# A softmax's first store moved from SyncE's queue of transfers to ScalarE's

## The chip, the cores and the metric

One core of one Trainium2 chip. The metric is the device time of one execution in microseconds (us), given as the median of the runs. The other cores are idle.

## The reference

A softmax over the last axis with temperature 2, on 16 x 1024 rows of 512 float32 values:

```python
def reference(x):                       # (16, 1024, 512) float32
    x_scaled = x / 2.0
    x_max = np.max(x_scaled, axis=-1, keepdims=True)
    exp_x = np.exp(x_scaled - x_max)
    return exp_x / np.sum(exp_x, axis=-1, keepdims=True)
```

33.55 MB come in and 33.55 MB go out. With 128 partitions there are 128 rows of 2 KB for each partition.

## The kernel before

All 128 rows per partition are cut into nine tiles of 3, 5, 9, 15, 21, 31, 15, 17 and 12 rows, and these into 23 chunks. A tile is the unit of a transfer, a chunk that of the arithmetic. The packet records have 144 records for each transfer: 128 packets, one per partition with all the tile's rows of that partition (6 to 62 KB), 8 for each of the core's 16 DMA engines, and 16 completions. The transfers of one queue wait in line; this line is called the ring below. An arena of 99 rows holds them; tiles 7 and 8 take the places of earlier ones and wait for their stores. VectorE finds the maximum, ScalarE does the exponential in place and the sum, VectorE takes the reciprocal and multiplies, two chunks behind its maximum. One queue, SyncE's, issues every load and store in a fixed order:

```python
PLAN = [                                # (rows of the chunks of a tile), place in the arena
    ([3], 0), ([5], 3), ([5, 4], 8), ([5] * 3, 17), ([7] * 3, 32), ([8, 8, 8, 7], 53),
    ([5] * 3, 84), ([6, 6, 5], 0), ([4] * 3, 17),
]
QUEUE = [
    ("load", 0), ("load", 1), ("load", 2), ("load", 3), ("load", 4), ("load", 5),
    ("load", 6), ("store", 0), ("store", 1), ("store", 2), ("store", 3), ("load", 7),
    ("store", 4), ("load", 8), ("store", 5), ("store", 6), ("store", 7), ("store", 8),
]
...
            if kind == "load":
                for u in behind.get(t, []):              # tiles whose place it takes
                    nc.sync.wait_ge(st[u], stored[u])
                ... nc.sync.dma_start(out=arena[...], in_=dram(xf, t)[...]).then_inc(ld[t], 16)
                continue
            ...
            nc.sync.wait_ge(s_mul, k + 1)                # the tile's last chunk is multiplied
            ... nc.sync.dma_start(out=dram(of, t)[...], in_=arena[...])
...
        for k, (t, b, c, a) in enumerate(chunks):        # ScalarE
            for r in range(c):
                ins = nc.scalar.activation(... Exp, bias=negmax, scale=0.5, accum_out=sums ...)
                if r == 0:
                    ins._wait_ge(s_max, k + 1)
            ins.then_inc(s_exp, 1)
        for k in range(len(chunks) + LAG):               # VectorE, LAG = 2
            if k < len(chunks):
                do_max(k)
            if k >= LAG:
                do_mul(k - LAG)
```

The softmax here doesn't subtract the row's maximum and nothing guards it: scores larger than these inputs give would overflow.

## Time and profile before

| | before |
|---|---|
| time, median of the 3 runs known at the prediction | 163.24 us (162.96 to 163.44) |
| span of the profiled run | 161.1 us |
| VectorE busy, ScalarE busy | 125.1 us, 94.0 us |
| transfers, all on one queue | 67.11 MB, 97.8% of 16 engines' span |

The list of transfers (what, queue, size, us from issue to landing) has store 0 and load 7:

```profile
out_dram<-arena SPq DMA_DIRECT2D x1, 768.0 KB, 49.0
arena<-in_x_dram SPq DMA_DIRECT2D x1, 4352.0 KB, 19.7
```

Store 0 is on its way for 49 us, because loads 4 to 6 (17.6 MB) and the rest of load 3 stand ahead of it in the same ring. And the chain of who waited for whom has for VectorE (us in total, times, longest):

```profile
DVE negmax L115 <- DMA arena<-in_x_dram: 9.0, 4, 4.5
```

VectorE waits for a load four times, all before 22.2 us, and never again.

### The profile page before, as it was taken

The numbers are of one execution on the slowest core, as the hardware profiler recorded it, in microseconds if no ns is written. First come the engines' busy times: TensorE is split into PE (matmuls) and PEld (weight loads), VectorE is DVE, ScalarE is ACT, GpSimd is POOL, SyncE is SP. The second block draws the span as 40 slices with busy tenths as digits, with TensorE's granted clock in tenths as the row PEclk, the third lists the DMA queues.
The fourth block names the chain that finished last, engine by engine and source line by source line (L and its number), as shares of the span: only waits on it lengthen the run. The fifth ranks groups of instructions, "written<-read, shape, count | busy, mean of one in ns | idle before, by whom it ended". The sixth has DMA issues, their size and how long they took to land.

```text
span 161.1 us, 494 instructions
## 1 busy us (share of the span) xinstructions
DVE 125.1 (78%) x174; ACT 94.0 (58%) x257; POOL 0.2 (0%) x4
## 2 busy tenths in 40 slices
DVE  0557989999999999999999999999999994000000
ACT  3455957674977949696977764697875770000000
POOL 0000000000000000000000000000000000000000
DMA  7999999997996998999999989899899979999991
GB/s 264 458 476 397 458 404 480 450 490 331 504 473 286 458 397 292 458 433 458 419 413 458 480 382 491 363 416 552 349 457 489 426 340 458 409 439 415 420 464 61
DMA packets 2595, 67.13 MB, mean 417 GB/s; under 512 B 288, under 2 KB 288, under 8 KB 544
## 3 DMA queue, kind: packets, MB, share of 16 engines
q1 hardware_dynamic: 2592, 67.11, 97.8%
q14 instruction: 3, 0.02, 0.0%
HBM read 33.55 MB, written 33.55 MB: 416 GB/s over the span
## 4 chain that ended last, share of the span: by engine, by line
DVE 69%; DMA 13%; issue 0%; DVEq 0%; SPq 0%
DVE negmax L115 38%; DVE arena L128 30%; DMA arena<-in_x_dram 13%; DVE recip L124 1%; DVEq L209 0%; SPq L100 0%
## 5 line engine op out<-in xcount | busy, mean ns | idle before, releaser
L141 ACT ACTIVATE arena<-arena,negmax 128x512 f32<-128x512 f32 x128 | 90.7, 709 | 37.1 <-DVE negmax L115 37.1
L115 DVE TENSOR_REDUCE negmax<-arena 128x5 f32<-128x2560 f32 (+5 forms) x23 | 71.7, 3116 | 9.0 <-DMA arena<-in_x_dram 9.0
L128 DVE TENSOR_SCALAR arena<-arena,recip 128x512 f32<-128x512 f32 x128 | 52.8, 482 | 0.8
L141 ACT ACTIVATION_READ_ACCUMULATOR arena<-arena,negmax 128x1 f32 x128 | 23.9, 187 | 0.0
L124 DVE RECIPROCAL recip<-sums 128x5 f32<-128x5 f32 (+5 forms) x23 | 4.2, 181 | 0.0
L141 ACT ACT_TABLE_LOAD x1 | 1.3, 1283 | 1.3 <-PEq L198 1.3
L198 POOL MEMSET const-bfloat16-1.0<- 128x1 bf16 x1 | 0.1, 101 | 0.0
L198 POOL MEMSET const-uint8-127<- 128x1 uint8 x1 | 0.1, 101 | 0.0
L198 POOL MEMSET const-float32-0.0<- 128x1 f32 x1 | 0.1, 98 | 0.2 <-issue 0.2
L198 POOL MEMSET const-float32-1.0<- 128x1 f32 x1 | 0.1, 98 | 0.0
## 6 DMA issues: line engine op xcount, KB each, us to landing
arena<-in_x_dram SPq DMA_DIRECT2D x1, 7936.0 KB, 50.9
out_dram<-arena SPq DMA_DIRECT2D x1, 7936.0 KB, 36.5
arena<-in_x_dram SPq DMA_DIRECT2D x2, 3840.0 KB, 40.8
out_dram<-arena SPq DMA_DIRECT2D x2, 3840.0 KB, 32.5
arena<-in_x_dram SPq DMA_DIRECT2D x1, 5376.0 KB, 32.4
out_dram<-arena SPq DMA_DIRECT2D x1, 5376.0 KB, 32.0
arena<-in_x_dram SPq DMA_DIRECT2D x1, 4352.0 KB, 19.7
out_dram<-arena SPq DMA_DIRECT2D x1, 4352.0 KB, 25.5
```

Source lines behind the costliest of these rows:

```text
L115: nc.vector.reduce_max(out=negmax[:, b : b + c], in_=arena[:, a : a + c], axis=mybir.AxisListType.X, negate=True,)._wait_ge(ld[t], loads_o ...
L124: nc.vector.reciprocal(out=recip[:, b : b + c], in_=sums[:, b : b + c])._wait_ge(s_exp, k + 1).then_inc(s_rec, 1)
L128: ins = nc.vector.tensor_scalar_mul(out=arena[:, a + r], in0=arena[:, a + r], scalar1=recip[:, b + r : b + r + 1],)
L141: ins = nc.scalar.activation(out=arena[:, a + r], in_=arena[:, a + r], func=mybir.ActivationFunctionType.Exp, bias=negmax[:, b + r : b + r ...
L198: nc = _bacc.Bacc("TRN2", target_bir_lowering=False, num_devices=1)
```

## The change

Store 0 need not stand for 45 us behind loads (its first packet starts at 62.6 us). It goes to ScalarE's queue, issued in ScalarE's program after chunk 2's exponentials, so that it runs while SyncE's queue still loads. Its early landing would also be one thing less ahead of load 7. The diff, cut to its core (`do_store` is the old store code with the engine as an argument):

```diff
-    ("load", 6), ("store", 0), ("store", 1), ("store", 2), ("store", 3), ("load", 7),
+    ("load", 6), ("store", 1), ("store", 2), ("store", 3), ("load", 7),
...
+SIDE = {2: 0}
...
+    def do_store(engine, t, lo, hi, groups):
+        ...
+        engine.wait_ge(s_mul, k + 1)
+        ... engine.dma_start(out=dram(of, t)[...], in_=arena[...]) ...
...
             ins.then_inc(s_exp, 1)
+            if k in SIDE:
+                do_store(nc.scalar, SIDE[k], 0, tiles[SIDE[k]][1], [(0, P, 1)])
```

More of the change, by code (lines that the diff above doesn't have):

```diff
@@ L90 @@
             loads_of[t] = loads_of.get(t, 0) + 16 * (len(rest[2]) if rest else 1)
+    def do_store(engine, t, lo, hi, groups):
+        b, r, at = tiles[t]
+        k = max(k for k, c in enumerate(chunks) if c[0] == t and c[1] - b < hi)
+        engine.wait_ge(s_mul, k + 1)
+        for p, q, step in groups:
+            u = t if t in awaited else "end"
+            engine.dma_start(
+                out=dram(of, t)[p:q:step, lo:hi], in_=arena[p:q:step, at + lo : at + hi, :]
+            ).then_inc(st[t] if t in awaited else s_end, 16)
+            stored[u] = stored.get(u, 0) + 16
     def do_queue(items):
@@ L94, in do_queue @@
             b, r, at = tiles[t]
-            lo, hi, groups = rest if rest else (0, r, [(0, P)])
-            if kind == "load":
-                for u in behind.get(t, []):
-                    nc.sync.wait_ge(st[u], stored[u])
-                for p, q in groups:
-                    nc.sync.dma_start(
-                        out=arena[p:q, at + lo : at + hi, :], in_=dram(xf, t)[p:q, lo:hi]
-                    ).then_inc(ld[t], 16)
+            lo, hi, groups = rest if rest else (0, r, [(0, P, 1)])
+            if kind == "store":
+                do_store(nc.sync, t, lo, hi, groups)
                 continue
-            k = max(k for k, c in enumerate(chunks) if c[0] == t and c[1] - b < hi)
-            nc.sync.wait_ge(s_mul, k + 1)
-            for p, q in groups:
-                u = t if t in awaited else "end"
+            for u in behind.get(t, []):
+                nc.sync.wait_ge(st[u], stored[u])
+            for p, q, step in groups:
                 nc.sync.dma_start(
-                    out=dram(of, t)[p:q, lo:hi], in_=arena[p:q, at + lo : at + hi, :]
-                ).then_inc(st[t] if t in awaited else s_end, 16)
-                stored[u] = stored.get(u, 0) + 16
+                    out=arena[p:q:step, at + lo : at + hi, :],
+                    in_=dram(xf, t)[p:q:step, lo:hi],
+                ).then_inc(ld[t], 16)
     def do_max(k):
```

## The prediction

> **What bounds the kernel now.** I read the page's summary first, then the SyncE queue's own waits, then the engines' order of time around 19 us (where the moved store will land), then stretches of the DMA traffic, and last the trace's packet records.
>
> The page, busy shares, the 40 slices and the queues:
>
> ```profile
> span 161.1 us, 494 instructions
> DVE 125.1 (78%) x174; ACT 94.0 (58%) x257; POOL 0.2 (0%) x4
> ...
> DVE  0557989999999999999999999999999994000000
> ...
> DMA  7999999997996998999999989899899979999991
> ...
> q1 hardware_dynamic: 2592, 67.11, 97.8%
> ```
>
> VectorE stops at slice 34, but the DMA row stays at 9 from slice 2 to slice 39: one queue, 97.8% of the 16 engines' span, carries all 67.11 MB. The 2592 packets are 18 transfers of 144 (128 rows of one partition each, and 16 completions). The packet records agree: from 2 to 156 us the number in flight is 16.0 in every 2 us stretch, so every engine moves one packet after the other with no gap. The sum of packet times over 16 engines is 157.8 us. This kernel is bound by transfers; VectorE is not.
>
> The page's chain of what ended last names VectorE all the same (69%), because it ends with the last multiply:
>
> ```profile
> 133.19 0.49 DVE arena L128
> 133.68 0.40 DVEq L209
> 134.07 0.79 DVE arena L128 x2
> ```
>
> That is 134.86 us; the span is 161.1. After it come 26 us of stores already queued or issued at once. So the chain is a false lead here: VectorE may slip until the queue would run dry. Store 8 is issued at 134.89 us, and store 7 ends at 152.5 us (packet records): 17 us in hand. Store 5 is issued at 96.94, and load 8 ahead of it ends at 114.4: again 17 us.
>
> The SyncE queue's own waits:
>
> ```profile
> SPq L108 <- DVE arena L128: 93.3, 8, 16.6
> SPq L98 <- DMA out_dram<-arena: 25.8, 1, 25.8
> SPq L209 <- PEq L209: 25.6, 2, 25.1
> SPq L100 <- DMA out_dram<-arena: 7.8, 1, 7.8
> ```
>
> They look large, but cost nothing: SyncE waits while earlier transfers still run. The 25.8 us are load 7's wait for stores 0 to 2 (it goes out at 74.94 us); store 3, 3.93 MB, is still in the ring and keeps the engines busy until 83.6 us.
>
> One place does lose time. Stretches of 2 us (engine busy times, clock, DMA share, GB/s):
>
> ```profile
> 52.40:54.40 2.00, 1.97 (x7) 1.92 (x5) 0.00 (x0) 1.00 1.07 461
> 54.40:56.40 2.00, 2.00 (x4) 2.00 (x7) 0.00 (x0) 1.00 1.03 445
> 56.40:58.40 2.00, 2.00 (x1) 1.12 (x4) 0.00 (x0) 1.00 1.10 476
> 58.40:60.40 2.00, 1.97 (x4) 0.59 (x1) 0.00 (x0) 1.00 0.96 323
> 60.40:62.40 2.00, 2.00 (x7) 2.00 (x7) 0.00 (x0) 1.00 0.97 246
> 62.40:64.40 2.00, 2.00 (x2) 2.00 (x7) 0.00 (x0) 1.00 0.76 316
> 64.40:66.40 2.00, 2.00 (x1) 1.16 (x4) 0.00 (x0) 1.00 1.09 461
> ```
>
> From 59 to 64 us the engines are busy but slow. The packet records put it down to the last two packets per engine of load 6, just ahead of store 0, the kernel's first store: the 128 packets of load 6 take 1.292 us in the mean against a median of 1.138, so 8 x 0.154 = 1.23 us per engine are lost. The next two passages from a load to a store (load 7 to store 4, load 8 to store 5) lose 0.13 and 0.05 us, and those from a store to a load nothing. Why the first one is dear the trace doesn't say; that it is the first store of the kernel is my guess, by likeness to load 0, whose first packets are also slow (0.287 us mean against 0.234 median, 0.43 us per engine).
>
> **What the Trainium skill says.** "DMA: Bandwidth & Descriptors", section "Issuing engines are not separate DMA queues": transfers from SyncE and ScalarE end up on the same 16 DMA engines and interleave; a second issuer saves only issue time. The trace agrees as far as it can with one queue: an issue on SyncE takes 0.33 to 0.81 us and all lie beside transfers, so there is no issue time to save. Same page, section "Queues, rings and completion order": each engine goes round robin between the rings that have work, packet by packet. Nothing in the trace before shows this; I use it for how the moved store shares with the loads. "HBM Reference", section "Specifications (TRN2)": a core that streams alone measures about 425 GB/s, bounded by its DMA engines. Here 67.11 MB in 157.8 us are 425 GB/s, so there is no idle bandwidth for a second queue to fill.
>
> **The change part by part.** *Taken off SyncE's queue:* store 0, 3 rows of 2 KB in 128 partitions, 0.79 MB. Its 8 packets per engine take 0.234 us each, 1.87 us. Before, it waited in the ring behind loads 3 to 6 from its issue at 17.31 us and landed after 66 us (49.0 us later).
>
> *Put on ScalarE:* one wait for the first chunk's multiply and one issue, between chunk 2 and chunk 3 of the exponentials.
>
> ```profile
> 15.80 0.17 DVE L124 RECIPROCAL recip<-sums 128x3 f32<-128x3 f32 x1
> 16.00 1.28 DVE L128 TENSOR_SCALAR arena<-arena,recip 128x512 f32<-128x512 f32 x3
> 19.51 0.72 ACT L141 ACTIVATE arena<-arena,negmax 128x512 f32<-128x512 f32 x1
> 25.03 0.72 ACT L141 ACTIVATE arena<-arena,negmax 128x512 f32<-128x512 f32 x1 [2.59 <-DVE negmax L115]
> ```
>
> The multiply is done at 17.28 us, ScalarE reaches the issue at about 19.5, so the wait is already met. The issue costs some 0.35 us (SyncE's for the same store took that), perhaps 0.8. Chunk 3 then starts late by that much, but ScalarE stands idle for 2.59 us before chunk 4: it is absorbed, 0 us on the path.
>
> *Moved:* the store's 8 packets per engine now slip between the 30 KB packets of load 3 (1.138 us each) and the 42 KB packets of load 4 (1.589 us), from about 20 us on. Load 3 ends at 21.7 us; at most two packets per engine of it remain, so it lands 2 x 0.234, about 0.5 us, later. VectorE waits for it at 22.18 us (0.50 us of idle before), so its chain slips by about 0.5 us, against 17 us in hand: 0. Loads 4 to 6 land up to 1.87 us later. Load 4's landing moves from 34.4 to 36.3 us, wanted at 36.57; load 5's from 53.4 to 55.3, wanted at 55.37 (and these wants slip by the same 0.5); load 6's from 64.1 to 66, wanted at 84.97. No new wait.
>
> *Unchanged:* the bytes ahead of store 2 in the rings are the same (loads 0 to 6 and stores 0 to 2), so store 2 lands at 74.5 us and load 7 is released as before; all behind it keeps its place. Sum of the direct costs: 0.0 us.
>
> *What is left is the 1.23 us at the first passage to a store.* It may stay where it is, before store 1 (0). It may go with the first store to about 20 us, where an engine held up is held up for either ring (0 again). Or it is hidden because the other ring's packets go on during the hold-up: up to -1.2. Against it, up to eight alternations of load and store per engine could each cost what a later passage cost, 0.05 to 0.13 us: +0.4 to +1.0. I give the hiding a little under one half and the alternation cost a third: 0.45 x -1.2 + 0.33 x 0.5 = about -0.4 us. From 163.24: 162.8.
>
> **The rivals.** *Gain of 1 to 1.5 us*, as above, 161.8 to 162.3: for it speaks that the slow stretch ends exactly at the first store; against, that an engine has no gap, so a second ring can only help if the delay belongs to a ring and not to the engine. *Loss by alternation*, 163.6 to 164.3, if mixed reading and writing slows packets; the cheap later passages speak against it. *A new wait on VectorE* (load 4 or 5 late): harmless to the end, as it would have to exceed 17 us. *ScalarE held up long at the issue* because the rings are full of loads: SyncE issued store 0 into the same full rings in 0.35 us, so unlikely; it too would have to cost many us. *Faster by over 2%*, below 160.0: 67.11 MB at the median packet rate of the largest packets (63,488 bytes in 2.342 us, times 16: 434 GB/s) are 154.7 us, only 3.1 us under the 157.8, and 2% is 3.26 us; there is not enough to win.
>
> **Range and chances.** All courses lie between 161.7 and 164.3, most between 162 and 163.5; the runs of before spread by 0.5. Predicted 162.8, range 161.6 to 164.0. Faster by over 2%: 0.02; within 2%: 0.95; slower: 0.03, for an interleaving worse than any passage seen.
>
> **What would show it.** Right: a second queue with 144 packets, 0.79 MB; DMA share still near 98%; load 3 landing about 0.5 us later; store 0 landing some 12 us after its issue and not 49; load 7 still released near 75 us; ScalarE's idle time before chunk 4 shorter by the issue. The slow packets tell the rest: at 59 to 64 us still (no gain), at 20 us instead (moved), or in neither (hidden). Wrong: load packets between 20 and 35 us clearly over 1.138 and 1.589 us, a gap in the DMA row before 155 us, or a time outside the range.

## The result, and the profile after

163.12 us (median of 4 runs, 163.04 to 163.38) against 163.10 of the kernel before (now 4 runs, 162.92 to 163.44). The ratio is 1.0001, with a 95% interval of 0.998 to 1.0023: the same. Here and below, a ratio is the mean time of one kernel's fast runs over that of the other's of the same rounds, so not quite the ratio of the medians that are quoted.

The page of the changed kernel:

```profile
span 161.3 us, 494 instructions
...
DMA  7999999997999799999899989899989969999991
...
q1 hardware_dynamic: 2448, 66.32, 96.5%
q10 hardware_dynamic: 144, 0.79, 1.2%
```

The second queue has taken its 144 packets and 0.79 MB, and the two together (97.7%) keep the engines as busy as the one did (97.8%). The list of transfers, and VectorE's and SyncE's waits:

```profile
out_dram<-arena ACTq DMA_DIRECT2D x1, 768.0 KB, 19.7
...
arena<-in_x_dram SPq DMA_DIRECT2D x1, 4352.0 KB, 20.0
```

```profile
DVE negmax L122 <- DMA arena<-in_x_dram: 9.4, 4, 4.4
...
SPq L113 <- DMA out_dram<-arena: 24.9, 1, 24.9
```

Store 0 now lands 19.7 us after its issue, 29 us earlier than before. Nobody was waiting for it: load 7 waits for stores 0, 1 and 2, of which store 2 is the last, and it still goes out at 74.38 us (74.94 before). VectorE waits for load 3 for 1.00 us, where it was 0.50. In order of time, ScalarE around the issue (start, us, what):

```profile
17.24 0.37 ACTq L100 DMA_DIRECT2D out_dram<-arena  x1
17.27 0.70 ACT L148 ACTIVATE arena<-arena,negmax 128x512 f32<-128x512 f32 x1
...
19.44 0.72 ACT L148 ACTIVATE arena<-arena,negmax 128x512 f32<-128x512 f32 x1
```

The issue stands in the program after chunk 2's five exponentials, but it is executed at 17.24 us, as soon as the multiply is done, with three of the five still to start. Chunk 3's exponentials begin at 19.44 us (19.51 before): the issue cost ScalarE nothing.

The transfers around the first store that is left on SyncE's queue, in stretches of 2 us (the last two columns are DMA share and GB/s; a packet seems to count wholly in the stretch where it starts, so that shares can exceed 1):

```profile
58.40:60.40 2.00, 1.98 (x2) 0.09 (x1) 0.00 (x0) 1.00 1.14 492
60.40:62.40 2.00, 1.98 (x5) 2.00 (x6) 0.00 (x0) 1.00 0.85 323
62.40:64.40 2.00, 2.00 (x4) 2.00 (x7) 0.00 (x0) 1.00 0.93 271
```

The slow stretch is still there, at the end of load 6, 2 us later as load 6 is.

To follow it I use one measure from the packet records: for a load, the mean time of its 128 packets minus the median of packets of its size in the kernel before, times 8, as each engine moves 8 of them. I call it the load's loss. Load 6 had (1.292 - 1.138) x 8 = 1.23 us before and has (1.239 - 1.138) x 8 = 0.81 us now; load 3, beside which the first store is now issued, has (1.161 - 1.138) x 8 = 0.18, where it had none. So it was neither moved nor hidden as a whole. The measure scatters from trace to trace: the second trace of the kernel before (before_again, below) has 1.49 at load 6.

A second measure turned out to decide. Each of the 16 engines writes a completion when its share of a transfer is done. Those of the last store, store 8, tell when each engine is done with everything. The last of them is when the kernel's work ends:

| completions of store 8, us from the span's start | median engine | last engine | behind |
|---|---|---|---|
| before | 157.92 | 159.75 | 1.83 |
| changed | 157.75 | 159.86 | 2.11 |
| before, second trace (before_again) | 158.08 | 159.88 | 1.80 |

In the first two, twelve of the engines end within 1.2 us of each other, and the last one 1.3 us after those twelve. Two traces of one kernel differ by 0.16 us in the median and 0.13 in the last, so the differences between before and changed (0.17 and 0.11) are no larger than chance.

### The profile page after: what moved, and what is told of

It reads as the page before. It is cut to its first block, busy times and chain, and to the rows that moved or that the text cites. A ratio compares the mean times of both kernels' runs of the same rounds, so it can differ in the third digit from the quotient of the medians.

```text
span 161.3 us, 494 instructions
## 1 busy us (share of the span) xinstructions
DVE 125.1 (78%) x174; ACT 94.1 (58%) x257; POOL 0.2 (0%) x4
## 4 chain that ended last, share of the span: by engine, by line
DVE 69%; DMA 13%; issue 0%; DVEq 0%; SPq 0%
DVE negmax L122 38%; DVE arena L135 30%; DMA arena<-in_x_dram 13%; DVE recip L131 1%; DVEq L218 0%; SPq L115 0%
```

## The experiments

Three questions: does the queue or the place of store 0 matter; what is the slow stretch; and what, if not VectorE, sets the end? The expectations speak of theories A (narrow packets right behind a load are dear), B (the first store is dear) and C (the end of a long run of loads is dear) for the slow stretch. Twelve kernels ran, all with correct results. Some expectations give a loss or a lag by a slightly different count (1.24 us for wide_first's loss; lags of 0.9 and 1.5 us for side_all and the kernel before); by the two measures above these are 1.31, 0.98 and 1.83.

### before_again: the kernel before, once more

No edit.

> The kernel before, unchanged, for a second trace. If the slow stretch at 59 to 64 us is a property of the program, the last packets of load 6 again cost about 1.2 us per engine more than the median packet (1.23 in the first trace, 0.81 in the changed kernel's). If it is chance, they cost near 0 or sit elsewhere. Time 163.1 +- 0.4 either way.

Measured: 163.04 us in its one run. Load 6's loss is 1.49 us (1.23 in the first trace), the last engine 1.80 us behind the median one (1.83). Both came again, so they are properties of the program and not of one execution; their sizes scatter by some 0.3 and 0.1 us.

### sync_early: store 0 early, on SyncE's queue

```diff
-    ("load", 0), ("load", 1), ("load", 2), ("load", 3), ("load", 4), ("load", 5),
-    ("load", 6), ("store", 0), ("store", 1), ("store", 2), ("store", 3), ("load", 7),
+    ("load", 0), ("load", 1), ("load", 2), ("load", 3), ("store", 0), ("load", 4),
+    ("load", 5), ("load", 6), ("store", 1), ("store", 2), ("store", 3), ("load", 7),
```

> Store 0 on SyncE's one queue again, but issued early, between load 3 and load 4. Theory (the engines are never without a packet, so neither the queue nor the place of 0.79 MB matters): ratio 0.997 to 1.003, store 0 lands near 24 us, loads 4 to 6 land 1.9 us later as in the changed kernel. Rival (the second queue by itself costs or gains something that the early place gives back): ratio outside that band, or the sum of slow packets differs by over 0.5 us per engine from the changed kernel's 1.9.

Measured: 163.03 us, ratio 1.0003 (0.9986 to 1.0021). Stretches of it:

```profile
18.00:20.00 2.00, 1.97 (x4) 2.00 (x6) 0.00 (x0) 1.00 0.96 292
20.00:22.00 2.00, 1.59 (x5) 2.00 (x7) 0.00 (x0) 1.00 0.94 233
...
60.00:62.00 2.00, 1.97 (x3) 0.15 (x1) 0.00 (x0) 1.00 1.03 445
62.00:64.00 2.00, 2.00 (x6) 2.00 (x7) 0.00 (x0) 1.00 1.10 476
```

The slow stretch has gone from 59 to 64 us to 18 to 22 us, ahead of store 0's new place: load 3's loss is 1.37 us, load 6's is 0.00. The losses of all transfers together are 2.2 us, against 1.9 in the changed kernel, within the expected 0.5. Neither the queue nor the place of store 0 changes the time. Theory C falls: load 6 now ends a run of 17.6 MB of loads and loses nothing, load 3 one of 8.4 MB and loses 1.37 us. Theory B gains.

### wide_first and narrow_later: is it the width of the packets?

wide_first (store 3, with 30 KB packets, comes first after load 6) and narrow_later (6 and 10 KB packets follow load 7):

```diff
 # wide_first
-    ("load", 6), ("store", 0), ("store", 1), ("store", 2), ("store", 3), ("load", 7),
-    ("store", 4), ("load", 8), ("store", 5), ("store", 6), ("store", 7), ("store", 8),
+    ("load", 6), ("store", 3), ("store", 0), ("store", 1), ("store", 2), ("store", 4),
+    ("load", 7), ("load", 8), ("store", 5), ("store", 6), ("store", 7), ("store", 8),
 # narrow_later
-    ("store", 4), ("load", 8), ("store", 5), ("store", 6), ("store", 7), ("store", 8),
+    ("store", 4, 0, 3, [(0, 128)]), ("store", 4, 3, 8, [(0, 128)]),
+    ("store", 4, 8, 21, [(0, 128)]), ("load", 8), ("store", 5), ("store", 6), ...
```

> The kernel before, with store 3 (30 KB packets) ahead of stores 0, 1 and 2 (6 to 18 KB), and store 4 ahead of load 7 so that the ring doesn't run dry. Three theories of the slow last packets of load 6. A, narrow packets right behind a load are what is dear: the loss at 59 to 64 us falls to under 0.3 us per engine, time about 1 us less (ratio 0.993 to 0.997). B, the first store of the kernel is dear, of whatever width: loss stays at 0.8 to 1.2 us, ratio 1.00. C, a long run of loads ends dear whatever follows: as B. B is weakened already, as the changed kernel's first store is elsewhere and 0.81 of the loss stayed.

> The kernel before, with store 4 cut into 3, 5 and 13 rows, so that 6 KB and 10 KB packets follow load 7, where 42 KB packets followed and the loss was 0.13 us per engine. Theory A (narrow packets right behind a load): loss at the end of load 7, near 90 to 94 us, rises to 0.8 to 1.2 us, time up by about 1 us (ratio 1.004 to 1.008). B and C: loss there stays under 0.3, ratio 1.00 to 1.002.

Measured: wide_first 162.46 us, ratio 0.9962 (0.9948 to 0.9976). narrow_later 164.11 us, ratio 1.0067 (1.0048 to 1.0087). Both times lie where theory A put them, and theory A is nevertheless wrong: in wide_first load 6's loss is 1.31 us and not under 0.3, and in narrow_later load 7's is 0.07 us and not 0.8 to 1.2. Where the time went is seen only in the engines' ends:

| | median engine | last engine | behind |
|---|---|---|---|
| wide_first | 157.87 | 159.28 | 1.41 |
| narrow_later | 158.04 | 160.94 | 2.90 |

The median engine ends within 0.12 us of where it did before (157.92). The last one ends 0.47 us earlier and 1.19 us later, and the medians of the runs have moved by -0.59 and +1.06 (before: 163.05 on this chip). The end of the traffic, first of the kernel before, then of narrow_later:

```profile
156.00:158.00 2.00, 0.00 (x0) 0.00 (x0) 0.00 (x0) 1.00 0.83 356
158.00:160.00 2.00, 0.00 (x0) 0.00 (x0) 0.00 (x0) 1.00 0.09 37
160.00:162.00 2.00, 0.00 (x0) 0.00 (x0) 0.00 (x0) 1.00 0.00 0
```

```profile
156.00:158.00 2.00, 0.00 (x0) 0.00 (x0) 0.00 (x0) 1.00 0.86 369
158.00:160.00 2.00, 0.00 (x0) 0.00 (x0) 0.00 (x0) 1.00 0.26 111
160.00:162.00 2.00, 0.00 (x0) 0.00 (x0) 0.00 (x0) 1.00 0.03 12
```

After 158 us few packets are started, and in narrow_later for 1.2 us longer (the last one at 160.02 us, before at 158.83): some engines are still at their last packets while the others are done.

### loads_joined: one passage from loads to stores fewer

wide_first did two things. This takes one of them alone:

```diff
-    ("load", 6), ("store", 0), ("store", 1), ("store", 2), ("store", 3), ("load", 7),
-    ("store", 4), ("load", 8), ("store", 5), ("store", 6), ("store", 7), ("store", 8),
+    ("load", 6), ("store", 0), ("store", 1), ("store", 2), ("store", 3), ("store", 4),
+    ("load", 7), ("load", 8), ("store", 5), ("store", 6), ("store", 7), ("store", 8),
```

> The kernel before with only one thing of wide_first: store 4 goes ahead of load 7, so that loads 7 and 8 run back to back and the ring passes from loads to stores twice and not three times; stores 0 to 2 keep their place right behind load 6. wide_first was 0.6 us faster although its loss behind load 6 stayed (1.24 us per engine), so theory A is dead, and the gain must be at the end of the slowest engine (159.28 against 159.74 us, the median engine unchanged). If it comes from the passage left out: ratio 0.994 to 0.998. If it comes from the wide store's place after load 6: ratio 0.999 to 1.001.

Measured: 162.69 us, ratio 0.997 (0.9958 to 0.9982). The median engine ends at 157.92 as before, the last at 159.44 (before 159.75). Load 6's loss is 1.38 us. So wide_first's gain can be had, within the two intervals, from this reordering alone, which leaves a passage out.

### side_three and side_all: more of the change

```diff
 # side_three, against the changed kernel
-    ("load", 6), ("store", 1), ("store", 2), ("store", 3), ("load", 7),
+    ("load", 6), ("store", 3), ("load", 7),
-SIDE = {2: 0}
+SIDE = {2: 0, 3: 1, 5: 2}
 # side_all, against the changed kernel; store 8 is issued after the last exponential
-    ("load", 6), ("store", 1), ("store", 2), ("store", 3), ("load", 7),
-    ("store", 4), ("load", 8), ("store", 5), ("store", 6), ("store", 7), ("store", 8),
+    ("load", 6), ("load", 7), ("load", 8),
-SIDE = {2: 0}
+SIDE = {2: 0, 3: 1, 5: 2, 8: 3, 11: 4, 15: 5, 18: 6, 21: 7}
+        do_store(nc.scalar, 8, 0, tiles[8][1], [(0, P, 1)])
```

> The change tripled: stores 0, 1 and 2 (4.46 MB) on ScalarE's queue beside loads 4 to 6. Theory (transfers bound, queue irrelevant): ratio 0.997 to 1.003, load packets at their median of 1.589 and 2.342 us, loads 4 to 6 later by up to 10 us, VectorE waits for them but within its 17 us in hand. Rival (alternation of loads and stores on one engine costs 0.05 to 0.13 us each): 24 store packets per engine, 1 to 3 us more, ratio 1.006 to 1.02. Rival (a second queue gains): below 0.997.

> The change taken to its end: all nine stores on ScalarE's queue, all nine loads on SyncE's. Wrong for speed on purpose as to order: loads and stores share the engines from the start. If alternation costs nothing, packets keep their medians (1.138, 1.589, 2.342 us), the sum of packet times stays at 157.7 to 158.5 us over 16 engines, and the time can only rise by gaps, from VectorE starved of loads and the last store alone at the end: 163 to 172 us. If mixing is dear, the sum of packet times rises by over 2 us.

Measured: side_three 163.57 us, ratio 1.0019 (1.0001 to 1.0037), as the theory had it. side_all 162.26 us, ratio 0.9942 (0.9926 to 0.9958), below the expected 163 to 172: a miss. Packets keep their medians in both, but for load 5's (2.370 and 2.396 us against 2.342); the sum of all packet times over 16 engines is 157.7 and 157.4 us, not above the 157.8 of the kernel before. So alternation costs nothing in sum.

The loss is now paid in parts (load 5's includes its higher median). In side_three loads 3, 4 and 5 lose 0.22, 0.28 and 0.67 us and load 6 none; in side_all 0.13, 0.26 and 0.70, and load 6 none. Together that is 1.17 and 1.09 us, against 1.23 to 1.49 at load 6 in the two traces of the kernel before. The gain of side_all is again at the end: its median engine ends at 157.78, its last at 158.76, 0.98 us behind. With its loads and its stores in two rings, neither ring passes from loads to stores.

### side_joined: the changed kernel with the passage left out

The diff is that of loads_joined, made to the changed kernel.

> The changed kernel with store 4 ahead of load 7, as loads_joined did to the kernel before (0.997 there, slowest engine 159.43 against 159.74 us). If the passages of one ring from loads to stores are what makes single engines fall behind: ratio 0.995 to 0.998 again, with the first store on ScalarE's queue adding nothing. If loads_joined was a matter of its chip or of store 0's place: 0.999 to 1.002.

Measured: 162.22 us (161.76 to 162.89), ratio to the kernel before 0.9955 (0.9936 to 0.9973); median engine 157.87, last 159.40. The gain of loads_joined is there again, on another chip. Whether the change adds to it was not measured side by side; the intervals of side_joined and loads_joined overlap.

### side_late: only the later stores on ScalarE

```diff
-    ("load", 6), ("store", 1), ("store", 2), ("store", 3), ("load", 7),
-    ("store", 4), ("load", 8), ("store", 5), ("store", 6), ("store", 7), ("store", 8),
+    ("load", 6), ("store", 0), ("store", 1), ("store", 2), ("store", 3), ("load", 7),
+    ("load", 8),
-SIDE = {2: 0}
+SIDE = {11: 4, 15: 5, 18: 6, 21: 7}
+        do_store(nc.scalar, 8, 0, tiles[8][1], [(0, P, 1)])
```

> Stores 0 to 3 on SyncE's queue as before, stores 4 to 8 on ScalarE's. This keeps the dear first passage (load 6 to store 0) and takes away the two later ones, as load 7 and load 8 then stand in another queue than the stores. side_all was 0.58% faster with its slow packets down from 2.01 to 1.57 us per engine and its slowest engine 0.9 us behind the median one instead of 1.5. If its gain is the lag of the slowest engine: here 0.994 to 0.998 and a lag of about 1 us. If its gain is the first passage's loss being spread: here 0.999 to 1.001.

Measured: 167.61 us, ratio 1.0282 (1.0269 to 1.0295). Neither theory; the run can't tell them apart, because a third thing came in. Its waits, VectorE's and SyncE's:

```profile
DVE negmax L122 <- DMA arena<-in_x_dram: 27.2, 6, 16.8
...
SPq L115 <- DMA out_dram<-arena: 19.8, 1, 19.8
```

Store 4 goes out on ScalarE's queue at 70.19 us, 5 us before SyncE issued it in the kernel before, and takes every other packet from 74 us on. Store 3 shares with it and lands at 96.4 us instead of 83.6; load 7 stands behind store 3 and lands at 116.0 instead of 94.3; load 8 waits for store 3 (19.8 us where it was 7.8) and lands at 134.9 instead of 114.4. VectorE stands for 16.8 us. Here the second queue gave a store every other packet, though a load was more urgent.

### first_tiny: a very small first store

```diff
-    ("load", 0), ("load", 1), ("load", 2), ("load", 3), ("load", 4), ("load", 5),
+    ("load", 0), ("load", 1), ("load", 2), ("tiny", 8), ("load", 3), ("load", 4),
+    ("load", 5), ...                                 # the rest in the same order
...
+            if kind == "tiny":
+                nc.sync.wait_ge(s_spare, 1)          # zeros, from GpSimd
+                nc.sync.dma_start(out=dram(of, t)[:, 0, 0:128], in_=spare[:, :]).then_inc(s_tiny, 16)
+                continue
+            if kind == "store" and t == 8:
+                nc.sync.wait_ge(s_tiny, 16)
...
```

> The kernel before with a store of 512 B per partition (zeros, written over by store 8 later, which waits for it) on SyncE's queue between load 2 and load 3. If the loss of 1.23 us at the end of load 6 belongs to the first store of the queue whatever its size, it moves to the end of load 2 near 12 us and the end of load 6 loses under 0.3. If it needs a store of some size, it stays at 59 to 64 us. Time the same within 0.3% in either case.

Measured: 163.28 us, ratio 1.0028 (1.0008 to 1.0047). Load 2's loss is 0.15 us, load 6's 1.18. The loss stays: 64 KB of stores don't take it with them, 0.79 MB on the same queue did (sync_early). So theory B falls in its plain form, in which a first store of any size is dear.

### dve_20 and dve_52: how much is in hand on VectorE

```diff
+            if k == 14:
+                nc.vector.memset(spare[:, :], 1.0).then_inc(s_spare, 1)
+                for n in range(20):                  # 52 in dve_52
+                    nc.vector.tensor_scalar_mul(out=spare[:, :], in0=spare[:, :], scalar1=1.0
+                    )._wait_ge(s_spare, n + 1).then_inc(s_spare, 1)
```

> The kernel before with 20 idle multiplies of 128x512 on a spare tile put into VectorE after chunk 12's multiply (near 91 us), about 20 x 0.5 = 10 to 13 us of VectorE time. Theory (VectorE has 17 us in hand, the chain that names it is a false lead): time as before, ratio 0.998 to 1.003. Rival (VectorE bounds): 10 to 13 us more, ratio 1.06 to 1.08.

> As dve_20 (9.7 us more on VectorE, 0.3% more time), with 52 multiplies: 52 x 0.46 + 0.5 = 24.4 us more on VectorE. Store 5 then goes out at 96.9 + 24.4 = 121.3 us, the ring runs dry at 114.4: a gap of about 7 us in the DMA row near 115 to 121 us and 7 to 9 us more time, ratio 1.04 to 1.055. If VectorE had no 17 us in hand: 1.15. If it had far more: 1.00 to 1.01.

Measured: dve_20 163.80 us, ratio 1.0032 (1.0013 to 1.005), for this much more work on VectorE, in its order of time:

```profile
91.15 0.48 DVE L162 MEMSET spare<- 128x512 f32 x1
91.67 9.19 DVE L164 TENSOR_SCALAR spare<-spare 128x512 f32<-128x512 f32 x20
```

9.7 us of VectorE for about 0.5 us of time: the rival (1.06 to 1.08) is out. The ratio is just outside the expected 0.998 to 1.003; the trace has the median engine at 157.86 as before and the last at 160.50, 2.65 us behind. The order of transfers is the same. Its last engine fell 0.67 us further behind during store 6 (see below); why, no run says.

dve_52: 173.67 us, ratio 1.0652 (1.0638 to 1.0666), above the expected 1.04 to 1.055 and far under 1.15. Stretches of it:

```profile
112.00:114.00 2.00, 1.86 (x5) 0.00 (x0) 0.00 (x0) 1.00 0.23 98
114.00:116.00 2.00, 1.90 (x5) 0.00 (x0) 0.00 (x0) 1.00 0.00 0
...
120.00:122.00 2.00, 2.00 (x5) 1.97 (x6) 0.00 (x0) 1.00 0.00 0
122.00:124.00 2.00, 2.00 (x2) 0.00 (x0) 0.00 (x0) 1.00 1.19 508
```

The ring runs dry where it was foretold, from 114.5 to 122.2 us; a second gap of 1.5 us, before store 7 (151.0 to 152.5), was not foretold. Its engines end within 0.2 us of each other: after the second gap they all start together, and what they had fallen behind is gone (the last one was 1.74 us behind after load 8, 0.92 after store 5 and 0.09 after store 7).

## Why the prediction was right

It was right as to the time: 162.8 predicted with 161.6 to 164.0, measured 163.12, and "within 2%" had 0.95. That the direct costs are nil was right and is shown. The gain of 0.4 us did not come (163.12 against 163.10), and the range held both cases, so the number alone tests little.

- **The bound.** Transfers bound and VectorE doesn't, although the chain names it: shown. 9.7 us more on VectorE cost 0.5 us, and the ring ran dry only when 24 us were added, at the place that the 17 us in hand gave.
- **Store 0 off the path.** Shown: store 0 lands 29 us earlier, load 7 goes out 0.56 us earlier, the time is the same. sync_early has the same early place without the second queue, and the same time.
- **ScalarE.** Nothing lost, but for another reason than the one given. The prediction had the issue at 19.5 us, after chunk 2's exponentials, and 0.35 us absorbed in a later idle time. It was executed at 17.24 us beside them. "Perfetto Trace Analysis", section "Sequencer Loop", of the Trainium skill says that the sequencer pushes an engine's instructions into a queue and goes on; the trace agrees, and the prediction should have used it. ScalarE's idle time before chunk 4 did not become shorter by the issue, as foretold, but longer (3.09 us against 2.59), because load 3 came later.
- **Load 3 late by 0.5 us.** VectorE's maximum began 0.43 us later (22.61 against 22.18), so the size is right. The reason is so in part: no packet of store 0 started before 21.13 us, 3.9 us after the issue, and none ahead of a data packet of load 3; about three packets per engine of load 3 (1.138 us each) went first. Load 3's own slow packets made its last data 0.28 us later (22.00 us against 21.72). The rest is one packet of store 0 (0.234 us), which on 12 of the 16 engines went ahead of load 3's completion: the last completion came 0.24 us after the data, where it was 0.01. Then store 0's eight packets per engine alternated one for one with load 4's, which is why it landed 19.7 us after its issue and not the expected 12: 3.9 us, and then eight pairs of 1.589 + 0.234, 14.6 us, so 18.5 of the 19.7.
- **The 1.23 us at the first passage, the term that was mis-sized.** The prediction gave -0.4 us, mostly for hiding behind the other ring. Loads 3 and 6 together lose 0.99 us now and load 6 lost 1.23 before: 0.24 us less per engine, of which nothing reaches the end. Two steps failed: the hiding, as most of the loss stayed, and adding a mean over 16 engines to the end. The last engine counts, and it ended 0.11 us later. That the 1.2 us were not hidden is shown; that they became less is not, as two traces of the kernel before differ by as much (1.23 and 1.49 us).
- **The alternation cost (+0.2 in the sum)** is nil: even where all stores alternate with loads, the sum of packet times is 157.4 us, against 157.8 (side_all).

**What stays open.** First, why the passage to the stores costs an engine 1.0 to 1.5 us once. It goes with the first 0.79 MB of stores on the same queue (sync_early), it is not taken by 64 KB (first_tiny), it doesn't depend on the packets' width (wide_first, narrow_later), and it is paid in parts when the stores come by a second queue (the changed kernel, side_three, side_all). No run says what it is.

Second, why single engines fall behind. Leaving out a passage from loads to stores brings the last engine 0.3 us closer (loads_joined) and lowers the time by 0.3%; giving stores and loads a queue each brings it 0.85 us closer (side_all). But dve_20 and narrow_later have the same passages and a later last engine. The completions of the earlier transfers tell where it falls behind (last engine behind the median one, us, one trace each):

| after | load 0 | load 5 | load 6 | load 7 | load 8 | store 8 |
|---|---|---|---|---|---|---|
| before | 0.71 | 0.84 | 1.34 | 1.70 | 1.86 | 1.83 |
| changed | 0.64 | 0.80 | 0.93 | 1.56 | 2.11 | 2.11 |
| loads_joined | 0.91 | 0.66 | 1.39 | 1.36 | 1.52 | 1.52 |
| narrow_later | 0.64 | 0.94 | 1.56 | 1.57 | 2.93 | 2.90 |
| dve_20 | 0.69 | 0.93 | 1.39 | 1.56 | 2.00 | 2.65 |

The first load leaves 0.6 to 0.9 us. After it the lag grows at the ends of loads, by up to 1.23 us where a store follows in the queue, though not at each such end, and by up to 0.3 us before load 6, where only loads follow. In loads_joined a load follows load 7, and the lag doesn't grow there. Stores carry it on within 0.12 us, but for store 6 of dve_20 (1.98 to 2.65). narrow_later lost its time at load 8, whose followers its edit left alone, so not at the narrow packets themselves. What makes an engine slow at those ends stays open.

That the last engine ends the kernel is shown: the time of an execution is its last engine's end and 3.15 to 3.25 us more, in every traced one. (The time is that of the traced execution; the ratio is that of all runs.)

| | last engine ends, us | time of that execution, us | ratio |
|---|---|---|---|
| side_all | 158.76 | 161.96 | 0.9942 |
| wide_first | 159.28 | 162.44 | 0.9962 |
| side_joined | 159.40 | 162.59 | 0.9955 |
| loads_joined | 159.44 | 162.59 | 0.9970 |
| before | 159.75 | 162.92 | 1 |
| first_tiny | 159.79 | 162.96 | 1.0028 |
| sync_early | 159.85 | 163.02 | 1.0003 |
| changed | 159.86 | 163.04 | 1.0001 |
| side_three | 160.19 | 163.37 | 1.0019 |
| dve_20 | 160.50 | 163.75 | 1.0032 |
| narrow_later | 160.94 | 164.09 | 1.0067 |

Only first_tiny is out of line by its ratio, because the traced execution was the fastest of its four (162.96 to 163.88 us).

**A faster version.** side_all (162.26 us, 0.58% faster than before) and side_joined (162.22 us, 0.45%) both beat the two kernels, by less than the 2% that would be called faster. They ran on different chips and were not set against each other.

## What to carry to other kernels

When the DMA engines have a packet at every moment, moving a transfer to another queue changes who goes first; look for what waits on its landing, and if nobody does, expect next to nothing (here 1.0001; from 0.9942 to 1.0019 with more of the stores moved and no load held up for long). In such a kernel the end is that of the slowest of the 16 engines, so compare the engines' last completions before explaining tenths of a per cent by means or by the chain of waits. A second queue splits the engines packet by packet: give it a store only if the loads that share the time have slack, as side_late shows.

## What the Trainium skill lacked or had wrong

- "DMA: Bandwidth & Descriptors", "Queues, rings and completion order": taking turns by packets agrees (store 0's and load 4's packets, of one partition each, went one for one), but the page doesn't say that a ring can first go on for some packets: store 0's first packet started 3.9 us after its issue, behind all that was left of load 3's data.
- Same page, "Issuing engines are not separate DMA queues": that a second issuer saves only issue time agrees for the change (ratio 1.0001) but not in general. The order changes too: all stores on ScalarE's queue gave 0.9942, the later ones alone 1.0282.
- No page that I read says how far apart the 16 engines of one core end with equal bytes on SyncE's and ScalarE's queues: the last one ends up to 2.9 us behind the median one (narrow_later; 1.83 us in the kernel before), and this sets the end. After the second gap in the ring all 16 end within 0.2 us (dve_52).
- No page that I read: the passage from loads to the kernel's first large store costs an engine 1.2 to 1.5 us in the mean, with packets of 1.138 us taking up to 2.2 (the two traces of the kernel before).
